# A hybrid decoder layer in split fp32: two output column blocks by seven products, with their weight sums made during the attention heads

## The chip, the cores and the metric

The kernel runs on one core of one Trainium2 chip. Its time is the device time of one launch in microseconds (us); shown are medians over runs. A core has TensorE (PE, matmuls), VectorE (DVE), ScalarE (ACT), GpSimd (POOL) and SyncE (SP, which here only starts transfers). Each engine works through its own instructions in a fixed order and waits on semaphores of the others.

## The reference, cut to what matters

S = 256 tokens, D = 2048, 16 heads, everything fp32.

```python
h = rmsnorm(x, pre_norm_g); proj = h @ w_in            # q_a, c_kv, k_rope, z, four conv parts, g_mla, g_conv
q = rmsnorm(q_a) @ w_q_b; kv = rmsnorm(c_kv) @ w_kv_b  # 16 heads, 128 + 64 rope
attn = causal_softmax(q k^T) v * silu(z);  y_mla  = attn @ w_o_mla
conv = sum(conv_w[k] * shifted(c_gate * c_in))
y_conv = (b_gate * conv * silu(z_conv)) @ w_o_conv
merged = sigmoid(g_mla) * y_mla + sigmoid(g_conv) * y_conv
out = merged @ w_out
x = x + rmsnorm(out, post_norm_g)
```

## The kernel before, in words

**Split fp32.** A product of fp32 matrices is made as three matmuls of rounded parts: hi x hi, lo x hi, hi x lo. Weights arrive as *raw units* of 128x2048 fp32 (1 MB): 4 blocks of 128 rows by 512 columns. A unit is rounded by `split_act`: ScalarE copies it into the rounded type (`whi`, L265), VectorE subtracts that from the raw values (`wlo`, L266). This is done in two halves of 1024 columns, into five half-sized buffers each for `whi` and `wlo`. The unit then serves 24 matmuls of 128x512: two row tiles of 128 tokens times four row blocks times three. All matmuls go through one helper (L88), which keeps them in program order; so the order of TensorE is the order of the code.

**The order of the other engines.** A scheduler arranges the instructions that are not marked `keep_in_program_order` by a simulated timeline when the kernel is built; the compiled order is then fixed. Raw units are loaded on SyncE's queue, three ahead (`ahead`), into three raw buffers, and rounded one ahead.

**Stages.** (1) Latents of the queries and keys, to 53 us. (2) Sixteen heads, to 590 us. Each head takes four weight units for the convolution channels (`cv`), with gates `z` for every fourth head, query and key units (`qn`, `kn`, `qr`) for every second head, and value units (`vv`) for every fourth; scores `sc`, `sw`, softmax `p` on VectorE and ScalarE, the probabilities turned by a round trip through DRAM, rounded as `pt`, and the values `o`. A head is one pass of a loop that calls, at fixed places, a generator that makes other data a step at a time (`make_forms`, for the next stage). `at_f` and `cv_f` hold the attention and convolution results of all heads, of 16 blocks each, and fill up head by head; `at_both`, `cv_both` are their rounded forms. (3) The gates, 590 to 916 us: four sets, each of two column blocks of both weights by *seven products* instead of eight (Strassen's scheme in Winograd's form: sums of weight blocks times sums of activation blocks, the latter being the *forms*), mixed with plain units `sq` of the branch outputs. A set's units are summed in place by VectorE (L1272, 128x2048) and rounded as `shi`, `slo`. (4) The output projection with `w_out`, 916.35 to 1003.39 us: 16 raw units in four column blocks c = 0..3 of 512, two row tiles, in the order of `out_order`; the merged activations `m` come back from DRAM turned (`turned_m`) and are rounded as `m_both`. (5) The norm, the gain, the residual and the stores.

Of the kernel before, what the change touches and what calls it, by code (L numbers as in the profile page):

```python
# [18 lines left out]
P = 128  # L19
S = 256  # L20
# [62 lines left out]
def tile_layer(ctx: ExitStack, tc: tile.TileContext, xw, w0, xb, x, pos, pvec, post_g, wc, wz, wcv, wkr, wqk, wqr, wv, cwr, wsq, out):  # L83
# [60 lines left out]

    out_order = [(0, 0), (0, 1), (1, 0), (1, 1), (0, 2), (1, 2), (0, 3), (1, 3)]
    out_order += [(c, k) for c in (2, 3) for k in range(4)]
    u_out = {ck: add(wsq[4, ck[0], ck[1]]) for ck in out_order}

    raws, splits, early = {}, {}, {}
    done = {"raw": 0, "split": 0, "end": u_first[1] + 1}  # L150

    def load_raw(i):
        ap, w = plan[i]
        t = early.get(i)
        if t is None:
# [20 lines left out]
    def split_unit(i):  # L176
        t, w = raws.pop(i), plan[i][1]
        parts = []
        if i == u_kr:
            t = t[:, :w].rearrange("p (k c) -> p k c", k=KD)  # L180
            for h in range(2):
                both = wpool.tile([P, HALF], F32R, name=f"whi{i}_{h}", tag="whi", bufs=5)
                both = both[:, :].rearrange("p (k j c) -> p k j c", k=KD // 2, j=2)
                ks = slice(h * KD // 2, (h + 1) * KD // 2)
# [4 lines left out]
        if i <= u_qa[-1]:  # L189

            hi, lo = (wpool.tile([P, HALF], F32R, name=f"{o}{i}", tag=o, bufs=5) for o in ("whi", "wlo"))
            for j in range(2):
# [4 lines left out]
            splits[i] = [(hi, lo)]  # L197
            return
        for h in range(0, w, HALF):
            n = min(HALF, w - h)  # L200
            if u_out[3, 0] <= i < u_out[3, 3]:
                both = spool.tile([P, 2, HALF], F32R, name=f"whl{i}_{h}", tag=LAST[len(last_parts)], bufs=1)
                last_parts.append(both)
                hi, lo = both[:, 0, :], both[:, 1, :]
            else:
                hi = wpool.tile([P, HALF], F32R, name=f"whi{i}_{h}", tag="whi", bufs=5)
                lo = wpool.tile([P, HALF], F32R, name=f"wlo{i}_{h}", tag="wlo", bufs=5)
            split_act(hi[:, :n], lo[:, :n], t[:, h : h + n], i in (u_head[0][1], *u_first, *u_d[0][2][:2]), i in (u_grp["r", 0], u_grp["v", 0], u_head[0][0]))
            parts.append((hi, lo))
# [13 lines left out]
    def take(i):  # L223
        ahead(i)
        return pieces(splits.pop(i))
# [391 lines left out]
    def group_a(g, together=False):  # L617
# [251 lines left out]
    def make_forms():  # L869
# [49 lines left out]
        while True:  # L919
            yield  # L920

    form, sums = {}, {}

# [6 lines left out]

    form_steps = make_forms()
    tap, coming, ps_by_head = None, [], {}
# [12 lines left out]

    def turned_unit(far, both, first, tag=None, queue=nc.sync):

# [3 lines left out]
        def load():  # L951
            name = f"turned_{both.name}{first}"
            if tag:
# [13 lines left out]

        return [[load if i == 0 else None, split(i), None, None] for i in range(len(far))]

# [24 lines left out]
    for h in range(H):  # L994
# [73 lines left out]
        if h < H - 2:  # L1068
            next(form_steps)
        channels(h, 2)  # L1070
        if h < H - 2:
            next(form_steps)
        if h == H - 1:
            split_branch(1)
# [49 lines left out]
    spool = right.enter_context(tc.tile_pool(name="spool", bufs=1, side="right", reuse_waits="tile"))  # L1124
    LAST = ("f5", "f6", "rb0", "rc0", "rc1", "rb1")
    last_parts = []

# [122 lines left out]
    def paired(i, n, c, combine):  # L1250
# [14 lines left out]
        def split(name, u, src, plus, then):  # L1265
            def go():
# [4 lines left out]
                if plus:  # L1271
                    nc.vector.tensor_tensor(t[:, :], t[:, :], raw[plus][:, :], op=ALU.add)  # L1272
                out = []
                for h in range(2):
                    hi = wpool.tile([P, HALF], F32R, name=f"shi{i}_{name}{u}_{h}", tag="whi", bufs=5)
                    lo = wpool.tile([P, HALF], F32R, name=f"slo{i}_{name}{u}_{h}", tag="wlo", bufs=5)
                    split_act(hi[:, :], lo[:, :], t[:, h * HALF : (h + 1) * HALF])
                    out.append((hi, lo))
                if then:
                    add_by_transfer(raw[then[0], u], then[1], 2 + u)  # L1280
                return pieces(out)
            return go
# [91 lines left out]
    m_b = Late("m", lambda i: spool.tile([P, 4, 2 * S], F32R, name=f"m_both{i}", tag=M_TAGS[i], bufs=1))  # L1374
    m_load = [turned_unit(far_m[a:b], m_b, a, tag, nc.gpsimd) for a, b, tag in ((0, 2, "rc0"), (2, 3, "rc1"), (3, 4, "rb1"))]

# [60 lines left out]
    loads.sort(key=lambda l: (max(l[1], -1), l[0]))  # L1437
    ns = 0
    ready = {}
    for j in range(-1, len(seq)):  # L1440
        while loads and loads[0][1] <= j:
            loads.pop(0)[2]()
        if j < 0:
            continue
        while ns < min(j + 3, len(seq)):
            ready[ns] = seq[ns][1]()
            ns += 1
        now[0] = j
# [3 lines left out]
        w = ready.pop(j)  # L1452
        if seq[j][2]:
            seq[j][2](w)
        for fn in pending.pop(j, []):
# [10 lines left out]
    assert not wanted and not fetched  # L1466

    m_load[1][0][0]()
    last_m = m_load[2][0]
# [9 lines left out]

    pss = [[bank(f"out{c}_{t}") for t in range(NT)] for c in range(2)]  # L1480
    for i, (c, kk) in enumerate(out_order[:4]):
        w = take(u_out[c, kk])
        if i == 0:
            last_m[0]()
        elif i == 2:
            m_load[1][0][1]()
        out_products(pss[c], w, kk)
    main.close()


    op = ctx.enter_context(tc.tile_pool(name="op", bufs=1))
    xr = op.tile([P, NT, D], F32, name="xr")
    og = op.tile([P, NT, D], F32, name="og")
    gb = op.tile([P, D], F32, name="gb")
    nc.scalar.dma_start(out=gb[:, :], in_=post_g.to_broadcast([P, D]))

    def out_block(c, t, ps):
# [5 lines left out]
        og_now = nc.vector.tensor_tensor(og[:, t, cs], ps[:, :], gb[:, cs], op=ALU.mult)  # L1503
        if c == 3:
            tc.keep_in_program_order(og_now)

# [48 lines left out]

    for i, (c, kk) in enumerate(out_order[4:6]):
        w = take(u_out[c, kk])
        if i == 0:
            last_m[1]()
        out_products(pss[c], w, kk)  # L1560
    tc.keep_in_program_order(nc.sync.dma_start(out=xr[:, :, :], in_=x))
    for c in range(3):
        if c == 2:
            pss.append([bank(f"out{c}_{t}") for t in range(NT)])
        for kk in range(4) if c == 2 else (3,):
            out_products(pss[c], take(u_out[c, kk]), kk)
        for t in range(NT):
            out_block(c, t, pss[c][t])
    nc.vector.reduce_sum(part[:, :], ssq[:, :, :3], axis=mybir.AxisListType.X)
    nc.vector.tensor_scalar(part[:, :], part[:, :], 1.0 / D, EPS, op0=ALU.mult, op1=ALU.add)  # L1570
    pss = [bank(f"out3_{t}") for t in range(NT)]
    for t in range(NT):
        for kk in range(4):
            if t == 0:
                last.append(take(u_out[3, kk]))
            out_products(pss, last[kk], kk, (t,))
        ps = out_block(3, t, pss[t])
        finish_by_two(t, ps) if t else finish(t)
# [90 lines left out]
```

## Time and profile before

| | |
|---|---|
| median of 3 runs | 1013.83 us (1013.68 to 1014.23) |
| the profiled execution | 1013.55 us, span 1011.8 us |
| granted TensorE clock | 0.998 |
| busy share of the span | PE 99%, DVE 80%, ACT 58%, POOL 17% |
| DMA | 261.84 MB, mean 259 GB/s |
| last output matmul ends | 1003.4 us; the end is the norm and the stores |

How to read the rows: in a group row, the line, the engine, the operation, out<-in with shape and count, then "busy us, mean ns of one", then the idle time of the engine just before them and what ended it. A timeline row has its start, its duration, the engine and what ran ("x2" joins two in a row), and in brackets the idle time before it with its cause. A window row has its limits, its length, the busy time of the engine asked for with the count of instructions, the granted clock, the share of the DMA engines and GB/s. Matmul rows overlap: the next starts before the end of the one before.

### The profile page before, as it was taken

To read this page: it belongs to the slowest core of one execution; us is meant where nothing else is said; L and a number is where in the kernel's file an instruction comes from. 1 tells how busy PE (TensorE), PEld (TensorE's weight loads), DVE (VectorE), ACT (ScalarE), POOL (GpSimd) and SP (SyncE) were. 2 spreads that over 40 slices of the span, in tenths; PEclk is the share of its full clock that TensorE was granted. 3 is DMA by queue.
4 is the path that set the end of the run, shared out by engine and by line. 5 is a ranking of instruction groups with operands and counts; after the bars stand their busy time and mean duration, and the time that the engine had idled before them with its cause. 6 is when DMAs were issued, how large, how long until landed. Compare 5 with 4: busy or idle time off the path is not lost.

```text
span 1011.8 us, 12983 instructions
## 1 busy us (share of the span) xinstructions
PE 1004.2 (99%) x4552; PEld 835.4 (83%) x4552; DVE 811.4 (80%) x1111; ACT 586.3 (58%) x838; POOL 170.7 (17%) x311
## 2 busy tenths in 40 slices
PE   9999999999999999999999999999999999999997
PEld 7888888888888888888888888888888888888886
DVE  7588878868888689877797889898989779997562
ACT  7675656556556456555565465565675664674541
POOL 4620411113211223212133110000000001003000
PEclk9999999999999999999999999999999999999999
DMA  8785768568786668866689779897599989639742
GB/s 338 282 291 183 260 201 304 197 214 276 234 303 232 228 229 283 272 219 232 216 264 338 292 306 291 344 375 218 187 333 296 305 321 260 239 127 322 289 166 84
DMA packets 54369, 261.84 MB, mean 259 GB/s; under 512 B 8768, under 2 KB 13504, under 8 KB 29216
## 3 DMA queue, kind: packets, MB, share of 16 engines
q1 hardware_dynamic: 37728, 214.35, 57.7%
q0 software_dynamic: 12256, 38.13, 14.0%
q10 hardware_dynamic: 4320, 8.54, 2.4%
q8 instruction: 35, 0.57, 0.2%
q14 instruction: 30, 0.25, 0.1%
HBM read 234.80 MB, written 22.02 MB: 254 GB/s over the span
## 4 chain that ended last, share of the span: by engine, by line
PE 98%; DMA 1%; DVE 0%; ACT 0%; SPq 0%; issue 0%
PE cv L88 34%; PE sq L88 17%; PE sX L88 9%; PE z L88 9%; PE out L88 9%; PE sZ L88 4%; PE kn L88 2%; PE qn L88 2%; PE vv L88 2%; PE sY L88 2%; PE ckv L88 2%; PE qa L88 2%; PE qr L88 1%; PE o L88 1%; PE sw L88 1%; DMA raw<-xb_dram 1%
## 5 line engine op out<-in xcount | busy, mean ns | idle before, releaser
L265 ACT ACTIVATE whi<-raw 128x1024 fp32r<-128x1024 f32 (+1 forms) x302 | 306.1, 1028 | 236.7 <-PE cv L88 103.9
L266 DVE TENSOR_TENSOR wlo<-raw,whi 128x1024 fp32r<-128x1024 f32 (+1 forms) x300 | 352.7, 1188 | 101.2 <-ACT whi L265 74.6
L88 PE MATMUL cv<-whi,x_both 128*128 128x512 f32 x1024 | 319.8, 389 | 0.0
L88 PEld LDWEIGHTS cv<-whi,x_both 128*128 128x128 f32 x1024 | 192.3, 188 | 39.5
L88 PE MATMUL cv<-wlo,x_both 128*128 128x512 f32 x512 | 199.5, 390 | 0.0
L88 PEld LDWEIGHTS cv<-wlo,x_both 128*128 128x128 f32 x512 | 96.2, 188 | 19.4
L266 DVE TENSOR_TENSOR slo_V<-b,shi_V 128x1024 fp32r<-128x1024 f32 x60 | 71.5, 1218 | 15.9 <-PE sq L88 8.5
L265 ACT ACTIVATE shi_V<-b 128x1024 fp32r<-128x1024 f32 x60 | 61.5, 1053 | 39.2 <-PE sq L88 21.2
L88 PE MATMUL z<-whi,x_both 128*128 128x512 f32 x256 | 80.0, 389 | 0.0
L366 POOL DMA_DIRECT2D far<-via x64 | 35.4, 559 | 227.2 <-DVE via L358 217.2
L88 PE MATMUL sq<-whi,at_both 128*128 128x512 f32 x256 | 60.6, 389 | 0.0
L88 PE MATMUL sq<-whi,cv_both 128*128 128x512 f32 x256 | 60.6, 389 | 0.0
L88 PEld LDWEIGHTS sq<-whi,cv_both 128*128 128x128 f32 x256 | 48.0, 188 | 10.0
L88 PEld LDWEIGHTS sq<-whi,at_both 128*128 128x128 f32 x256 | 48.0, 188 | 10.0
L88 PEld LDWEIGHTS z<-whi,x_both 128*128 128x128 f32 x256 | 48.1, 188 | 9.9
L88 PE MATMUL z<-wlo,x_both 128*128 128x512 f32 x128 | 49.8, 389 | 0.0
L88 PE MATMUL out<-whi,m_both 128*128 128x512 f32 x208 | 49.4, 389 | 0.0
L88 PE MATMUL sX<-shi_V,form 128*128 128x512 f32 x192 | 47.4, 389 | 0.0
L88 PEld LDWEIGHTS out<-whi,m_both 128*128 128x128 f32 x208 | 39.0, 188 | 8.1
L88 PEld LDWEIGHTS sX<-shi_V,form 128*128 128x128 f32 x192 | 36.0, 188 | 7.5
L265 ACT ACTIVATE shi_Q<-b 128x1024 fp32r<-128x1024 f32 x28 | 28.8, 1052 | 21.5 <-PE sq L88 19.1
L1263 POOL DMA_DIRECT2D b<-wsq_dram x8 | 7.0, 869 | 193.4 <-DVE b L1272 76.8
(304 smaller groups left out, 1568.7 us busy)
## 6 DMA issues: line engine op xcount, KB each, us to landing
raw<-wcv_dram SPq DMA_DIRECT2D x64, 1024.0 KB, 6.2
raw<-wsq_dram SPq DMA_DIRECT2D x48, 1024.0 KB, 7.2
b<-wsq_dram SPq DMA_DIRECT2D x26, 1024.0 KB, 5.7
raw<-wz_dram SPq DMA_DIRECT2D x16, 1024.0 KB, 4.9
raw<-wqk_dram SPq DMA_DIRECT2D x8, 1024.0 KB, 6.8
b<-wsq_dram POOLq DMA_DIRECT2D x8, 1024.0 KB, 11.0
far_form<-form ACTq DMA_DIRECT2D x28, 256.0 KB, 3.3
form<-far_form SPq DMA_DIRECT2D x7, 1024.0 KB, 13.8
```

Source lines behind the costliest of these rows:

```text
L88: return tc.keep_in_program_order(nc.tensor.matmul(*a, **kw))
L265: a = nc.scalar.activation(hi, src, AF.Copy)
L266: b = nc.vector.tensor_tensor(lo, src, hi.bitcast(F32), op=ALU.subtract)
L366: tc.keep_in_program_order(queue.dma_start(out=f[i], in_=m))
L1263: tc.keep_in_program_order(nc.gpsimd.dma_start(out=dst[:, :], in_=wsq[n, c + b, k], accum_op=ALU.add))
```

## The change

*Output projection.* Column blocks c = 1 and 2 are now made together by seven products (Q1, V5, V6, V7, V3, V4, Q2), each of two units of 12 matmuls, in three accumulators X, Z, Y. V5, V6, V7, V4 use weight sums. The activations' side needs four sums of `m` (the m forms V7, V5, V6, V3), made singly by VectorE and ScalarE in this stage. `out_order` has 22 units instead of 16; 8 of them are read from the weight sums (`far_sum`).

*Weight sums* (`make_sums`). Between heads 1 and 6, one step at each of three places in a head: 16 loads of 0.5 MB on SyncE's queue, 16 VectorE additions of 128x1024, 16 stores of 0.5 MB to DRAM on ScalarE's queue. They work in the quarters of `at_f` and `cv_f` that the heads have not filled yet.

*Whole-unit roundings.* From the end of the heads on, a unit is rounded by one ScalarE and one VectorE instruction of 128x2048 instead of two of 1024, in an area of five half slots used in turn; a pair that wraps takes slots 0 and 4. Only the first plain unit of the gate stage (raw115) is still rounded in halves, the first before the last head's values, the second after.

*Order.* In the gate stage the matmuls of a unit are issued before the rounding of the unit two ahead. In the first head the value unit no longer draws the rounding of the next unit (raw20) ahead. In the output stage five raw units are loaded ahead, six through a second area (`spare`), and all roundings are kept in program order. The rows `m2` and `m3` share a buffer, and the residual `xr` is loaded late.

Where the compiled order moves, before and after. Numbers at the end of names differ between the builds; `wlo_86` and `whi_85` are the five-slot areas.

VectorE, first head, from the rounding of the queries on. Before:

```order
L434 TENSOR_TENSOR f_867<-qn0_1_843,half_868 128x256
L266 TENSOR_TENSOR wlo20_0_874<-raw20_828,whi20_0_873 128x1024
L266 TENSOR_TENSOR wlo20_1024_878<-raw20_828,whi20_1024_877 128x1024
L266 TENSOR_TENSOR qn_lo_853<-f_863,qn_hi_852 128x256
L266 TENSOR_TENSOR qn_lo_853<-f_867,qn_hi_852 128x256
L434 TENSOR_TENSOR f_903<-kn0_0_885,half_904 128x256
```

After:

```order
L558 TENSOR_TENSOR f_867<-rp_a_871,rp_b_872 128x256
L312 TENSOR_TENSOR qr_862<-f_867,qr_862 64x256 x2
L312 TENSOR_TENSOR wlo_86<-raw20_784,whi_85 128x1024 x2
L312 TENSOR_TENSOR vv_lo_884<-vv0_0_889,vv_hi_883 128x512
L312 TENSOR_TENSOR vv_lo_884<-vv0_1_904,vv_hi_883 128x512
L312 TENSOR_TENSOR wlo_86<-raw21_821,whi_85 128x1024 x2
```

The roundings of raw20 have moved from ahead of the queries and keys to behind the rotated queries (`qr`).

VectorE, heads 5 to 6, from the queries to the rounded keys (`kn_... <- f_...`) of the next pair of heads. Before:

```order
L266 TENSOR_TENSOR wlo56_0_2785<-raw56_2698,whi56_0_2784 128x1024
L266 TENSOR_TENSOR qn_lo_2646<-f_2656,qn_hi_2645 128x256
L266 TENSOR_TENSOR qn_lo_2646<-f_2662,qn_hi_2645 128x256
L434 TENSOR_TENSOR f_2686<-kn3_0_2668,half_2687 128x256
L434 TENSOR_TENSOR f_2692<-kn3_1_2669,half_2693 128x256
L806 SCALAR_TENSOR_TENSOR cv_f_110<-cv5_0_2499,r_both_97,cv_f_110 128x512
L266 TENSOR_TENSOR kn_2647<-f_2686,kn_2647 128x256
L266 TENSOR_TENSOR kn_2647<-f_2692,kn_2647 128x256
L266 TENSOR_TENSOR wlo56_1024_2789<-raw56_2698,whi56_1024_2788 128x1024
```

After (L987 are the weight sums):

```order
L312 TENSOR_TENSOR wlo_86<-raw56_2557,whi_85 128x1024
L480 TENSOR_TENSOR f_2545<-kn3_0_2527,half_2546 128x256
L312 TENSOR_TENSOR wlo_86<-raw56_2557,whi_85 128x1024
L852 SCALAR_TENSOR_TENSOR cv_f_120<-cv5_1_2367,r_both_107,cv_f_120 128x512
L312 TENSOR_TENSOR qn_lo_2505<-f_2521,qn_hi_2504 128x256
L944 TENSOR_TENSOR form12_1_2668<-x_area_951,form12_1_2668 128x2x128
L937 TENSOR_TENSOR form_sum0_952<-x_area_951 128x256
L987 TENSOR_TENSOR cv_f_120<-at_f_119,cv_f_120 128x1024
L312 TENSOR_TENSOR kn_2506<-f_2545,kn_2506 128x256
```

The second half of raw56, two form steps and a weight sum now stand ahead of the first rounded keys; five more sums stand in the 44 rows before these.

ScalarE, end of the heads and start of the gate stage; `first_rt` are the first set's weights, which V5 adds to, `at_both3` the last quarter of the rounded attention result. Before:

```order
L811 ACTIVATE cg_5723<-cv15_1_5542,r_both_97 128x512
L265 ACTIVATE whi115_0_5729<-raw115_5727 128x1024
L265 ACTIVATE whi115_1024_5733<-raw115_5727 128x1024
L265 ACTIVATE at_both3_5747<-at_f_109 128x4x128 x2
L265 ACTIVATE whi116_0_5814<-raw116_5789 128x1024
L265 ACTIVATE whi116_1024_5818<-raw116_5789 128x1024
L1310 ACTIVATE sa0_5834<-sX0_5798 128x512
L265 ACTIVATE whi117_0_5838<-raw117_5791 128x1024
L265 ACTIVATE whi117_1024_5842<-raw117_5791 128x1024
L265 ACTIVATE whi118_0_5874<-raw118_5811 128x1024
L265 ACTIVATE whi118_1024_5878<-raw118_5811 128x1024
L265 ACTIVATE shi0_V50_0_5910<-first_rt0_5283 128x1024
```

After:

```order
L857 ACTIVATE cg_5351<-cv15_1_5194,r_both_107 128x512
L311 ACTIVATE whi_85<-raw115_5355 128x1024
L311 ACTIVATE at_both3_5369<-at_f_119 128x4x128 x2
L311 ACTIVATE whi_85<-raw115_5355 128x1024
L311 ACTIVATE whi_85<-raw116_5411 128x2048
L1402 ACTIVATE sa0_5452<-sX0_5420 128x512
L311 ACTIVATE whi_85<-raw117_5413 128x2048
L311 ACTIVATE whi_85<-first_rt0_4951 128x2048
L311 ACTIVATE whi_85<-raw118_5435 128x2048
```

`at_both3` has moved between the halves of raw115, and V5's rounding (of `first_rt0`) ahead of raw118's.

The diff, cut to its core:

```diff
@@ rounding of a unit @@
+    PARTS = 5
+    part_area = {o: wpool.tile([P, PARTS, HALF], F32R, name=o) for o in ("whi", "wlo")}
+    def unit_part(o):
+        a, b = sorted((part_n[o] + j) % PARTS for j in range(2))
+        part_n[o] += 2
+        return part_area[o][:, a : b + 1 : b - a, :]
...
+        if i == u_d[0][2][0]:
+            for h in range(len(halves[i]), 2):
+                if h == 0 or not only_first:
+                    hi, lo = half_part("whi"), half_part("wlo")
+                    split_act(hi, lo, t[:, h * HALF : (h + 1) * HALF], keep)
...
+        if i >= u_first[0]:
...
+                hi, lo = unit_part("whi"), unit_part("wlo")
+            split_act(hi[:, :, :], lo[:, :, :], t[:, :].rearrange("p (h s) -> p h s", h=2), keep, later)
@@ first head @@
-            ahead(u_grp["v", 0])
+            ahead(u_grp["v", 0], split=0)
@@ weight sums, one step a yield @@
+        for i in range(4):
+            bring(i, (3,))
+            plus(a, a, b)
+            yield
+            plus(b, b, c)
+            put(i, (1,))
+            yield
+            plus(c, a, c)
+            put(i, (0,))
+            if i < 3:
+                bring(i + 1, (0, 1))
+            yield
+            plus(d, c, d)
+            put(i, (2, 3))
+            if i < 3:
+                bring(i + 1, (2,))
+            yield
@@ a head, three places @@
             next(form_steps)
+            next(sum_steps)
@@ last head @@
-            split_unit(done["split"])
-            done.update(raw=done["raw"] + 1, split=done["split"] + 1)
+            split_unit(done["split"], True)
+            done["raw"] += 1
             finish_all(values(h, pt))
@@ output stage @@
+    def m_sum(i, j, x, y, op):
+        o = m_sums[:, i, 4 * j : 4 * j + 4, :]
+        tc.keep_in_program_order(nc.vector.tensor_tensor(quarters(o), x, y, op=op))
...
+    then((0, 0), last_m[0])
+    then((0, 1), form_of("V7"))
+    then((3, 0))
+    then(("Q1", 0))
+    then(("Q1", 1), lambda: m_load[1][0][1](True))
+    then((0, 2), form_of("V5"))
+    then(("V5", 0), lambda: last_m[1](True))
+    then(("V5", 1))
+    then((0, 3), lambda: copied("a", "X", "d"), form_of("V6"))
+    then(("V6", 0), lambda: copied("c", "Z", "a"))
+    then(("V6", 1), lambda: out_block(0, 0, pss[0][0]))
+    then((3, 1), lambda: out_block(0, 1, pss[0][1]))
+    then(("V7", 0), lambda: copied("b", "X", "b"), form_of("V3"))
+    then(("V7", 1))
+    then(("V3", 0))
+    then(("V3", 1), lambda: added("c", "X"))
+    then(("V4", 0), lambda: out_block(2, 1, res["c"], -1.0))
+    then(("V4", 1), lambda: added("b", "Z"), get_xr)
+    then(("Q2", 0), lambda: out_block(2, 0, res["b"], -1.0))
+    then(("Q2", 1), lambda: out_block(1, 1, set_bank["X"]))
```

Here `then(unit, steps)` first rounds the next unit (`take`), then does the steps, then issues the matmuls of the unit.

More of the change, by code (lines that the diff above doesn't have):

```diff
@@ L189, in split_unit @@
         if i <= u_qa[-1]:
-            hi, lo = (wpool.tile([P, HALF], F32R, name=f"{o}{i}", tag=o, bufs=5) for o in ("whi", "wlo"))
+            hi, lo = (half_part(o) for o in ("whi", "wlo"))
             for j in range(2):
@@ L223, in take @@
     def take(i):
-        ahead(i)
+        ahead(i, raw=5 if i >= u_out[0, 0] else 3)
         return pieces(splits.pop(i))
@@ L920, in make_forms, with make_sums, bring, put @@
             yield
+    def make_sums():
+        keep = tc.keep_in_program_order
+        area = [f[:, 4 * i : 4 * i + 4, :].rearrange("p k s -> p (k s)") for f in (at_f, cv_f) for i in (2, 3)]
+        a, b, c, d = area
+        w = 4 * S
+        def bring(i, which):
+            u, h = divmod(i, 2)
+            for n in which:
+                blk, k = ((1, u), (2, u), (2, 2 + u), (1, 2 + u))[n]
+                keep(nc.sync.dma_start(out=area[n], in_=wsq[4, blk, k][:, h * w : (h + 1) * w]))
+        def put(i, which):
+            u, h = divmod(i, 2)
+            for n in which:
+                keep(nc.scalar.dma_start(out=far_sum[("V5", "V7", "V6", "V4")[n], u][:, h * w : (h + 1) * w], in_=area[n]))
+        def plus(o, x, y):
+            keep(nc.vector.tensor_tensor(o, x, y, op=ALU.add))
+        for _ in range(3):
+            yield
+        bring(0, (0, 1))
+        bring(0, (2,))
+        yield
[10 more added lines that the diff above has]
+                bring(i + 1, (0, 1))
+            yield
+            plus(d, c, d)
+            put(i, (2, 3))
+            if i < 3:
+                bring(i + 1, (2,))
+            yield
+        while True:
+            yield
     form, sums = {}, {}
@@ L944, in score, with turned_unit @@
         return rest if later else rest()
-    def turned_unit(far, both, first, tag=None, queue=nc.sync):
+    def turned_unit(far, both, first, tag=None, queue=nc.sync, shared=None):
         box = []
@@ L966, in split @@
             return go
-        return [[load if i == 0 else None, split(i), None, None] for i in range(len(far))]
+        return [[load if i == 0 else None, split(i), None, None, box] for i in range(len(far))]
     def split_turned(src, both, t, keep=False):
@@ L1069, in tile_layer @@
             next(form_steps)
+            next(sum_steps)
         channels(h, 2)
@@ L1272, in go @@
                     nc.vector.tensor_tensor(t[:, :], t[:, :], raw[plus][:, :], op=ALU.add)
[L1273 to L1278, printed above, removed]
+                hi, lo = unit_part("whi"), unit_part("wlo")
+                split_act(hi[:, :, :], lo[:, :, :], t[:, :].rearrange("p (h s) -> p h s", h=2))
                 if then:
                     add_by_transfer(raw[then[0], u], then[1], 2 + u)
-                return pieces(out)
+                return pieces(by_halves(hi, lo))
             return go
@@ L1437, in tile_layer @@
     loads.sort(key=lambda l: (max(l[1], -1), l[0]))
-    ns = 0
-    ready = {}
+    ready = {ns: seq[ns][1]() for ns in range(2)}
+    ns = 2
     for j in range(-1, len(seq)):
@@ L1444, in tile_layer @@
             continue
+        w = ready.pop(j)
+        if seq[j][2]:
+            seq[j][2](w)
+        now[0] = j
         while ns < min(j + 3, len(seq)):
@@ L1478, in out_products @@
         ])
[L1480 to L1487, printed above, removed]
+    pss = {c: [bank(f"out{c}_{t}") for t in range(NT)] for c in (0, 3)}
+    m_raw = lambda blk, t: by_rows((m_01[0] if blk < 2 else pair_23)[:, (blk % 2) * 1024 + t * 512 :][:, :512], 4)
+    m_form = {n: spool.tile([P, KH, 2, P], F32R, name=f"m_form{n}", tag=tag, bufs=1) for n, tag in (("V5", "f5"), ("V6", "f6"), ("V7", "rb0"))}
@@ L1554, in finish_by_two @@
         store(t, 1536, 2048, og[:, t, cs])
[L1556 to L1568, printed above, removed]
+    res = {}
@@ new lines, in copied, with added, then @@
+    def copied(name, b, tag):
+        res[name] = wide(f"o{name}", tag)
+        tc.keep_in_program_order(nc.scalar.activation(res[name][:, :], set_bank[b][:, :], AF.Copy))
+    def added(name, b):
+        tc.keep_in_program_order(nc.vector.tensor_tensor(res[name][:, :], res[name][:, :], set_bank[b][:, :], op=ALU.add))
+    def then(n, *steps):
+        made = list(map(lambda f: f, steps))
+        c, k = n
+        w = take(u_out[n])
+        for f in made:
+            f()
+        if c in BANKS:
+            set_products(n, w)
+        else:
+            out_products(pss[c], w, k)
```

157 lines of the change are left out of this document (121 added, 36 removed).

## The prediction

> **What bounds the kernel now.** I read the page's busy shares first, then the waits of TensorE, then the chain of work that ended last, then the stretches around each edit.
>
> ```profile
> span 1011.8 us, 12983 instructions
> PE 1004.2 (99%) x4552; PEld 835.4 (83%) x4552; DVE 811.4 (80%) x1111; ACT 586.3 (58%) x838; POOL 170.7 (17%) x311
> q1 hardware_dynamic: 37728, 214.35, 57.7%
> PE 98%; DMA 1%; DVE 0%; ACT 0%; SPq 0%; issue 0%
> ```
> ```profile
> PE fin L88 <- ACT dg L1541: 0.9, 1, 0.9
> PE idle L88 <- PEq L1657: 0.8, 1, 0.8
> PE qa L88 <- ACT whi L265: 0.6, 2, 0.3
> ```
> ```profile
> 916.51 87.05 PE out L88 x384
> ```
>
> TensorE is the bound and waits 2.3 us in all, at the very start and end. The last row, of the chain, prices a matmul: 87.05 / 384 = 0.2267 us; a unit of 24 lasts 5.44, one of 12 lasts 2.72. So any matmul removed is worth 0.2267, and any work that comes late for TensorE is paid in full, unless it comes early enough to be hidden. Beside it VectorE is the fullest engine; its share of 80% is a mean, and the question is its queue where the change adds to it or reorders it.
>
> The prices of VectorE and ScalarE, by form:
>
> ```profile
> L266 DVE TENSOR_TENSOR wlo<-raw,whi 128x1024 fp32r<-128x1024 f32 x282 | 340.8, 1220 | 101.1 <-ACT whi L265 74.6 <-PE out L88 19.3 <-PE sY L88 1.8
> L1272 DVE TENSOR_TENSOR b<-b,b 128x2048 f32<-128x2048 f32 x16 | 36.5, 2283 | 0.3 <-DMA b<-wsq_dram 0.3
> L266 DVE TENSOR_TENSOR m_both<-turned_m,m_both 128x512 fp32r<-128x512 f32 x8 | 5.3, 684 | 1.4 <-ACT m_both L265 1.4
> L266 DVE TENSOR_TENSOR kn<-f,kn 128x256 fp32r<-128x256 f32 x16 | 6.3, 417 | 0.2 <-ACT kn L265 0.2
> L265 ACT ACTIVATE whi<-raw 128x1024 fp32r<-128x1024 f32 x282 | 294.0, 1057 | 233.0 <-PE cv L88 103.9 <-PE z L88 31.6 <-PE out L88 24.4
> ```
>
> Back to back each VectorE instruction starts about 0.08 before the one before ends (two 128x1024 in 2.34 to 2.36, quoted below), so in a queue a half costs 1.13 to 1.14, a whole 2.2, a 128x512 0.60, a 128x256 0.33. ScalarE's two halves take 1.99 together; a whole I estimate at 1.93.
>
> **The change, part by part.** I follow each engine's new order (the compiled orders, cut in the sections above) and put the durations of before on it. Times are those of before's trace.
>
> *Removed*: 384 matmuls of the output stage become 360: 24 x 0.2267 = **-5.44**. Nothing hides it; it is TensorE's own time.
>
> *A, first head.* The roundings of raw20 now stand behind the whole query and key chain on VectorE; before, they stood ahead of it.
>
> ```profile
> 81.01 2.34 DVE L266 TENSOR_TENSOR wlo<-raw,whi 128x1024 fp32r<-128x1024 f32 x2
> 89.13 0.87 DVE L266 TENSOR_TENSOR qr<-f,qr 64x256 fp32r<-64x256 f32 x2 [0.48 <-ACT qr L265]
> 87.34 0.39 PE L88 MATMUL cv<-wlo,x_both 128*128 128x512 f32 x1
> ```
>
> The chain ends at 90.0; with the two roundings (2.26) gone from ahead of it, at 87.7; the first half of raw20 then lands at 88.9 to 89.2, against 87.34: **+1.7** (0 if the scheduler's chain runs earlier, 2.3 if its keys wait).
>
> *B and D, the weight sums.* 16 additions of 128x1024 (16 x 1.13 = 18.1 us of VectorE) spread over heads 1 to 6. Nearly everywhere VectorE's gaps hide them. Not in front of the scores of head 6, which wait for the rounded keys:
>
> ```profile
> 245.00:274.29 29.29, 25.59 (x46) 1.00 0.71 245
> 272.41 0.75 DVE L266 TENSOR_TENSOR kn<-f,kn 128x256 fp32r<-128x256 f32 x2
> 274.26 0.28 PE L88 MATMUL sc<-kn,qn_hi 128*128 128x256 f32 x1
> ```
>
> (The first row is VectorE's busy time in a stretch.) Now stand ahead of the keys six sums (6.8) and, moved forward, half a rounding (1.13), two form steps (0.66) and a convolution product (0.66), less one 0.33: 8.9. The stretch has 29.29 - 25.59 = 3.7 idle, the lead of the keys included. 8.9 - 3.7 = 5.2 if every gap is filled; I take **+4.9**, since the chain there begins a little early (bounds 2, if half the sums slide into earlier gaps, and 7.5, if only the 1.4 of lead counts). B is a small one: one sum puts off a product that frees an accumulator in head 2, **+0.5** (0 to 1.1, one sum).
>
> *C, head 3.* The low part of the probabilities (pt) now stands behind both halves of raw44.
>
> ```profile
> 208.73 1.06 ACT L265 ACTIVATE whi<-raw 128x1024 fp32r<-128x1024 f32 x1 [3.01 <-PE z L88]
> 209.83 2.59 DVE L266 TENSOR_TENSOR wlo<-raw,whi 128x1024 fp32r<-128x1024 f32 x2 [2.85 <-ACT whi L265]
> 209.89 0.39 PE L88 MATMUL o<-pt,vv_hi 128*128 128x512 f32 x1
> ```
>
> In the new ring of five slots raw44's second half takes the slot that TensorE gives up at 208.7: ScalarE to 209.8, VectorE to 211.0, pt at 211.5, against 209.89: **+1.6** (0 to 3.1, the latter if the slot is the one that came free at 210).
>
> *E, end of the heads.* Only half of raw115 is rounded ahead of the last values; ScalarE does the second half behind at_both3, which waits for VectorE's at_f.
>
> ```profile
> 593.73 1.99 ACT L265 ACTIVATE whi<-raw 128x1024 fp32r<-128x1024 f32 x2
> 595.67 1.15 ACT L265 ACTIVATE at_both<-at_f 128x512 fp32r<-128x512 f32 x2
> 595.23 0.41 DVE L745 TENSOR_TENSOR at_f<-f,at_f 128x256 f32<-128x256 f32 x1
> 595.39 3.79 PE L88 MATMUL sq<-whi,at_both 128*128 128x512 f32 x16
> ```
>
> The second half is needed at the fifth of these matmuls, 596.3. at_f ended at 595.64 and is now about 1.1 later, because a whole rounding (2.2) stands where a half stood: 596.7 + 1.15 + 1.06 = 598.9, **+2.7** (1.5 if at_f is not later, 3.1 if it loses one thing more).
>
> *F.* ScalarE now rounds V5's sum ahead of raw118.
>
> ```profile
> 606.27 3.79 PE L88 MATMUL sq<-whi,at_both 128*128 128x512 f32 x16
> 605.97 4.48 DVE L1272 TENSOR_TENSOR first_rt<-first_rt,first_rb 128x2048 f32<-128x2048 f32 x2
> 611.71 3.79 PE L88 MATMUL sq<-whi,at_both 128*128 128x512 f32 x16
> ```
>
> V5's rounding takes a slot that TensorE gives up after 12 of the matmuls at 606.27, at 609.0; two whole units later (3.86) raw118 is there at 612.9, against 611.71: 1.2. VectorE follows with V5's low part, an addition (2.2) and only then raw118's: another 1.4. **+2.6** (1.2 to 3.9).
>
> *G, the gate stage.* Whole-unit roundings save VectorE some 0.07 each, but a unit's first half is ready 0.9 later on ScalarE and 1.1 later on VectorE.
>
> ```profile
> 850.00:900.00 50.00, 47.18 (x42) 1.00 0.65 208
> ```
>
> With 2.8 us free in 50 little is caught up. Following the order, two places come late, V4 of the second set (1.2) and V3 of the fourth (0.4): **+1.6** (0, the gain of VectorE covering it, to 3).
>
> *H, the output stage.*
>
> ```profile
> 916.00:960.00 44.00, 26.06 (x29) 1.00 0.84 306
> 960.00:1003.00 43.00, 21.44 (x26) 1.00 0.34 123
> ```
>
> VectorE had half its time free here; now it rounds 22 units instead of 16 and makes four forms (two 128x512 sums, 1.2, and a low part, 1.15, each, behind 1.06 of ScalarE). In the run of eight 12-matmul units (8 x 2.72 = 21.8) VectorE needs 8 x 2.2 + 2.35 + three additions and two gains (5 x 0.6) = 23.0. Each form is issued behind the next unit's rounding. V5's first unit starts at 916.35 + 27.2 = 943.6; its rounding waits for a slot until 937.2, ends on VectorE at 941.4, the sums at 942.6, ScalarE 943.7, the low part 944.9, against 943.8: 1.1. In the same way V6 0.9, V3 0.75 on ScalarE and 0.45 on VectorE, V4's first matmul 1.4 (its accumulator is read by an addition queued behind two roundings), small ones 0.3: **+4.9** (1.4, VectorE's excess alone, to 6.5).
>
> *DMA.* 6 MB more in the output stage fit the second row's share of 0.34. The sums add 16 loads and 16 stores of 0.5 MB (16.8 MB) to heads 1 to 6:
>
> ```profile
> 120.00:300.00 180.00, 145.97 (x247) 1.00 0.73 247
> raw<-wcv_dram SPq DMA_DIRECT2D x64, 1024.0 KB, 6.2
> ```
>
> q1 moved 214.35 MB in 57.7% of 1011.8 us, 367 GB/s, so they need 46 us of engine time; 0.27 x 180 = 49 is free. I cost it at nothing: a unit is asked for three units ahead (16.3 us) and lands in 6.2, so some 7 us of lead is left after both roundings. The price without that cover is the third rival.
> [...]
>
> Sum: 1.7 + 0.5 + 4.9 + 1.6 + 2.7 + 2.6 + 1.6 + 4.9 = 20.5; less 5.44: +15.1. The profiled execution took 1013.55, 0.3 under the median: **1028.6**.
>
> **Rivals.**
> *First, faster*: all waits are absorbed, since TensorE stalled nowhere before and a stall once paid gives every later queue its lead back; then only the 24 matmuls show: 1013.55 - 5.44 = 1008.1. For it: VectorE idles 20%. Against it: A, C, E and F are inversions in an order, not lack of throughput.
> *Second, no change*: only the inversions are real (A and C as costed, E and F at their low ends: 1.7 + 1.6 + 1.5 + 1.2 = 6.0) and the terms of load, D, G and H, vanish in gaps: 1013.55 - 5.44 + 6.0 = 1014.1. For it: the output stage's two rows show half of VectorE's time free. Against it: in front of the keys and in the gate stage the gaps are counted above and too short.
> *Third, slower still*: DMA saturates in heads 1 to 6. With 46 of 49 us taken, loads queue behind sums; it decides once a raw unit lands over 13 us after its issue. If a fifth of the 46 us reaches TensorE, 9 us: 1038.
>
> **How the numbers follow.** Forecast 0.58, first rival 0.12, second 0.13, third 0.17. The likeliest's own range, with the terms moving half independently, is 1022 to 1034. The range leaves out the first rival and the end of the third: **1013 to 1038**. About 0.2% (2 us) can be told from no change: faster 0.14 (the first rival and an edge of the second), same 0.06, slower 0.80.
>
> **What would show it.** Waits of TensorE by releaser in the profile after: one near 88 on VectorE's wlo, one near 212 on pt, the longest, near 280, on kn, one near 600 on ScalarE's whi, two on raw118, and five or six of about 1 us in the output stage on form parts; TensorE's last output matmul some 15 us later than 1003.4, with 24 fewer of them. I am wrong if TensorE's waits sum to under 6 us, if waits on DMA lead the list, or if the stall at kn is missing while DVE's sums are there.

## The result, and the profile after

The changed kernel takes 1036.1 us (median of 5, 1035.32 to 1038.91) against 1013.68 (1013.36 to 1014.23): 1.0226 times, 95% interval 1.0212 to 1.024, 22.4 us slower. The forecast was 1028.6, in a range of 1013 to 1038: direction and range held, the size was 15 of 22.

Two lines of the page, then TensorE's waits (engine, tile, releaser, us in total, times, longest):

```profile
span 1034.3 us, 12660 instructions
PE 1005.5 (97%) x4528; PEld 831.5 (80%) x4528; DVE 847.2 (82%) x1045; ACT 592.8 (57%) x748; POOL 170.9 (17%) x311
```
```profile
PE sc L88 <- DVE kn L312: 7.5, 1, 7.5
PE sq L88 <- ACT whi L311: 5.2, 3, 2.2
PE o L88 <- DVE pt L312: 1.6, 1, 1.6
PE cv L88 <- DVE wlo L312: 1.6, 1, 1.6
PE sq L88 <- DVE wlo L312: 1.5, 1, 1.5
PE out_setX L88 <- DVE oc L1711: 1.2, 1, 1.2
...
PE out_setZ L88 <- DVE m_formV L1595: 0.8, 1, 0.8
PE out_setX L88 <- DVE m_formV L1597: 0.8, 1, 0.8
PE out_setZ L88 <- ACT whi L311: 0.6, 1, 0.6
```

The waits are where the forecast put them: the keys (kn), pt, raw20's wlo, raw115 and raw118, the forms. Yet the listed waits come to some 21.7 us, less 5.4 for the matmuls: 16. The rest of the 22.4 is in PE's busy time. It rose from 1004.2 to 1005.5 with 24 matmuls fewer. So matmuls ran slower somewhere.

TensorE's order up to the output stage did not change, so the n-th matmul of one trace can be set against the n-th of the other. The growth of the difference of their starts, place by place (a restart costs 0.1 to 0.3 more than the wait in the list):

| place (time before) | forecast | measured | run that bears on it |
|---|---|---|---|
| A, raw20, 87 | 1.7 | 1.8 | e6 |
| B, head 2, 144 | 0.5 | 0.6 | e1, e3 |
| C, pt, 210 | 1.6 | 1.8 | e1 |
| D, keys of head 6, 274 | 4.9 | 7.6 | e1, e2, e3 |
| slow clock after D | none | 2.5 | e11, e12 |
| E, raw115, 596 | 2.7 | 2.5 | e6 |
| F, raw118, 612 | 2.6 | 3.2 | e4, e5 |
| G, V4 and V3 of the sets | 1.6 | 0.2 | |
| sq, 758 | none | 2.1 | e1, e2, e3 |
| H, output stage | 4.9 | 5.9 | e4 |
| 24 matmuls | -5.4 | -5.4 | |
| start of the latents, and small steps | none | -0.5 | |
| sum | 15.1 | 22.3 | |

The two profiled executions differ by 22.5 us. The start of the latents is a difference between launches: it is -0.9 in e12, whose code there is that of before.

*D and the clock.* TensorE's timeline at the keys, then the granted clock (the fourth number) in windows of TensorE:

```profile
285.52 0.58 PE L88 MATMUL sc<-kn,qn_hi 128*128 128x256 f32 x1 [7.47 <-DVE kn L312]
...
287.82 0.63 PE L88 MATMUL cv<-wlo,x_both 128*128 128x512 f32 x1
...
291.96 0.39 PE L88 MATMUL cv<-wlo,x_both 128*128 128x512 f32 x1
```
```profile
286.00:291.00 5.00, 5.00 (x15) 0.52 0.64 219
291.00:295.00 4.00, 4.00 (x19) 1.00 0.83 157
```

After the wait TensorE runs some 5 us at half clock (0.63 for a matmul that otherwise shows 0.39). That is the 2.5 us.

VectorE had the six sums in front of the keys, as forecast, but it also stood still there, for 3.0 us in one piece. ScalarE's timeline and, under it, SyncE's issues and VectorE's window (the last two numbers: DMA share, GB/s) and timeline:

```profile
262.76 1.06 ACT L311 ACTIVATE whi<-raw 128x1024 fp32r<-128x1024 f32 x1 [1.94 <-DMA raw<-wcv_dram]
...
271.84 2.01 ACT L311 ACTIVATE whi<-raw 128x1024 fp32r<-128x1024 f32 x2 [5.64 <-DMA raw<-wcv_dram]
```
```profile
256.95 1.06 SPq L979 DMA_DIRECT2D at_f<-wsq_dram  x2
260.87 0.33 SPq L198 DMA_DIRECT2D raw<-wcv_dram  x1
```
```profile
263.00:272.00 9.00, 6.92 (x10) 1.00 1.03 402
```
```profile
272.93 2.36 DVE L312 TENSOR_TENSOR wlo<-raw,whi 128x1024 fp32r<-128x1024 f32 x2 [3.01 <-ACT whi L311]
```

A raw unit asked for at 260.87, behind two loads of the sums, landed near 271.8: 11 us, against a median of 6.2 before, while the DMA engines were full (share 1.03). That is the third rival's mechanism, inside the forecast's own place. The loads of the sums stand in the raw units' own queue, ahead of this one. The stores are in ScalarE's queue, and they moved at the same time: while the unit was on its way (260.87 to 271.76), SyncE's queue moved 2.70 MB, ScalarE's 1.18 MB and GpSimd's 0.53 MB.

*The wait at 758* (the time before; 780 after) has a late transfer in it too, long after the sums. ScalarE's row of before, then two of after, and a VectorE window:

```profile
752.96 1.16 ACT L265 ACTIVATE cv_both<-turned_cv 128x512 fp32r<-128x512 f32 x2 [0.25 <-DMA turned_cv<-far_cv]
```
```profile
777.09 1.15 ACT L311 ACTIVATE cv_both<-turned_cv 128x512 fp32r<-128x512 f32 x2 [4.92 <-DMA turned_cv<-far_cv]
778.15 1.89 ACT L311 ACTIVATE whi<-raw 128x2048 fp32r<-128x2048 f32 x1
```
```profile
767.00:778.00 11.00, 9.61 (x9) 1.00 0.99 378
```

A raw unit's rounding stands on ScalarE behind cv_both, which waits for a transfer. Before, the first half of that unit stood ahead of it; a whole unit can't. Full DMA engines alone are not what is new: their share in this stretch was 1.01 before (746 to 757 us). But the two transfers landed 9.9 and 11.0 us after their issue, against 6.9 and 7.8 before. In the profiles of e1 and e2 they took 9.0 to 10.4 and the wait cost 1.3; in e3's they took 6.6 and 7.4 and there was no wait, though no edit of these three touches this place. Why the transfers are late is not shown.

### The profile page after: what moved, and what is told of

It is laid out like the page before. It is cut to its first block, busy times and chain, and to the rows that moved or that the text cites. A ratio compares the mean times of both kernels' runs of the same rounds, so it can differ in the third digit from the quotient of the medians.

```text
span 1034.3 us, 12660 instructions
## 1 busy us (share of the span) xinstructions
PE 1005.5 (97%) x4528; PEld 831.5 (80%) x4528; DVE 847.2 (82%) x1045; ACT 592.8 (57%) x748; POOL 170.9 (17%) x311
## 5 line engine op out<-in xcount | busy, mean ns | idle before, releaser
L311 ACT ACTIVATE whi<-raw 128x1024 fp32r<-128x1024 f32 (+2 forms) x260 | 303.6, 1177 | 226.5 <-PE cv L88 100.0
L312 DVE TENSOR_TENSOR wlo<-raw,whi 128x1024 fp32r<-128x1024 f32 (+2 forms) x258 | 352.7, 1375 | 91.2 <-ACT whi L311 86.0
L311 ACT ACTIVATE whi<-b 128x2048 fp32r<-128x2048 f32 x44 | 84.5, 1920 | 62.1 <-PE sq L88 37.2
L312 DVE TENSOR_TENSOR wlo<-b,whi 128x2048 fp32r<-128x2048 f32 x44 | 100.3, 2289 | 20.5 <-ACT whi L311 13.0
L88 PE MATMUL sX<-whi,form 128*128 128x512 f32 x256 | 63.3, 389 | 0.0
L88 PEld LDWEIGHTS sX<-whi,form 128*128 128x128 f32 x256 | 48.0, 188 | 10.0
L1368 DVE TENSOR_TENSOR b<-b,b 128x2048 f32<-128x2048 f32 x16 | 36.6, 2286 | 1.8 <-DMA b<-wsq_dram 1.6
L88 PE MATMUL sX<-wlo,form 128*128 128x512 f32 x128 | 34.3, 390 | 0.0
L88 PE MATMUL sq<-wlo,at_both 128*128 128x512 f32 x128 | 31.8, 390 | 1.5 <-DVE wlo L312 1.5
```

The costliest lines, as they stand in the source:

```text
L88: return tc.keep_in_program_order(nc.tensor.matmul(*a, **kw))
L311: a = nc.scalar.activation(hi, src, AF.Copy)
L312: b = nc.vector.tensor_tensor(lo, src, hi.bitcast(F32), op=ALU.subtract)
```

## The experiments

All are edits of the changed kernel but e11 and e12, which are edits of the kernel before. e1, e2, e3 and e10 leave out the sums or a part of them, so they give times and not the layer's result. Times of before in the three groups of runs: 1012.98, 1013.17, 1013.21.

**e1: no sums.**

```diff
-            u_out[n, k] = add(far_sum[n, k][:, :])
+            u_out[n, k] = add(wsq[4, 1 if n in ("V5", "V4") else 2, k])
...
-    form_steps, sum_steps = make_forms(), make_sums()
+    form_steps, sum_steps = make_forms(), iter(lambda: 0, 1)
```

> The changed kernel without the weight sums: nothing of them is loaded, added or stored during the heads, and the output stage reads a plain block of w_out in place of each sum. If the sums are what delays head 2, head 3 and head 6 (waits of TensorE that grew its lateness by 0.6, 1.8 and 10.1 us, the slowed clock behind the last one included), all three go: 1036.1 - 12.5 = 1023.6. If these waits come from the order of the roundings and not from the sums, they stay: 1036. The waits in the gate and output stages stay in both cases.

1023.33 (1.0097, 1.0082 to 1.0113). B, C and D are gone: no wait between 90 and 590 us. So pt (C), which I had put down to the new order of the roundings alone, came from the sums too: without them the compiled order rounds pt earlier again. A, E, F and H are about what they were, but for a stretch of slow clock behind E in this profile (more in the last section).

**e2 and e3: additions only, transfers only.** The first two edits are e2's (with e1's first), the last is e3's.

```diff
-                keep(nc.sync.dma_start(out=area[n], in_=wsq[4, blk, k][:, h * w : (h + 1) * w]))
+                pass
...
-                keep(nc.scalar.dma_start(out=far_sum[...][:, h * w : (h + 1) * w], in_=area[n]))
+                pass
...
         def plus(o, x, y):
-            keep(nc.vector.tensor_tensor(o, x, y, op=ALU.add))
+            pass
```

> Only the 16 additions of the weight sums are left; they add what happens to lie in the areas, no sum is loaded or stored, and the output stage reads plain blocks. VectorE's load alone (the forecast): TensorE waits 5 us for the keys of head 6, instead of 7.5; about 1031. If the transfers alone made the wait: under 1 us for the keys, about 1025.

> The 16 loads and 16 stores of the weight sums stay, the 16 additions are left out, so what is stored is not a sum. If VectorE's load alone makes the wait for the keys of head 6, it falls under 1 us: about 1024. If the saturated DMA engines make it, a raw unit still lands 10 us or more after its issue between 250 and 275 us, and the wait for the keys stays at 3 us or more: about 1028.

1031.87 (1.0191, 1.0162 to 1.0219; one of the four launches took 1037.08) and 1031.82 (1.0186, 1.0164 to 1.0208). TensorE's longest wait in each, then VectorE's windows in front of it:

```profile
PE sc L88 <- DVE kn L312: 5.9, 1, 5.9
```
```profile
250.00:270.00 20.00, 19.87 (x29) 1.00 0.70 235
```
```profile
PE sc L88 <- DVE kn L312: 4.7, 1, 4.7
```
```profile
255.00:263.00 8.00, 6.06 (x12) 1.00 0.97 369
263.00:272.00 9.00, 5.05 (x9) 1.00 1.03 422
```

With the additions alone VectorE is full (19.87 of 20) at a DMA share of 0.70: the forecast's mechanism, 5.9 where it said 4.9. With the transfers alone VectorE has 3.9 us of 9 free and the DMA engines none: the rival's mechanism, 4.7. Each alone delays the keys by 5 to 6 us and brings the slow clock (a mean of 0.98 from 120 to 300 us in both, where before has 1.00); together they give 7.5. The two don't add; I take it that they meet in the same stretch of VectorE's queue, which the one fills and the other stops. Neither expectation of "under 1 us" held. C is gone in both runs, so it needs the additions and the transfers; B is gone in e3 alone, so it comes from an addition.

**e4: halves from free buffers.**

```diff
-        k = part_n[o] % PARTS
         part_n[o] += 1
-        return part_area[o][:, k, :]
+        return wpool.tile([P, HALF], F32R, name=f"{o}_{part_n[o]}", tag=o, bufs=PARTS)
...
-                hi, lo = unit_part("whi"), unit_part("wlo")
-            split_act(hi[:, :, :], lo[:, :, :], t[:, :].rearrange("p (h s) -> p h s", h=2), keep, later)
+            for h in range(2):
+                hi, lo = half_part("whi"), half_part("wlo")
+                split_act(hi[:, :], lo[:, :], t[:, h * HALF : (h + 1) * HALF], keep, later)
```

> Every rounding is made in two halves again, from five half buffers given out as they come free; all else is as in the changed kernel. The forecast put the output stage's waits on forms that queue behind the next unit's rounding: by that they stay near 5.9 us, and so does raw118's (2 to 3), for some 1033. If the whole unit is the cause (it needs two slots at once and gives its first half late), the waits of raw118 (3.2), at 758 us (2.1) and of the output stage (5.9) shrink to 1.5 in all, E stays at 2.2: 1036.1 - 0.3 - 9.7 = 1026.

1025.3 (1.0117, 1.0094 to 1.014). What is left behind 590 us:

```profile
PE sq L88 <- ACT whi L314: 1.4, 1, 1.4
PE out_setX L88 <- DVE oc L1717: 1.1, 1, 1.1
...
PE out_setX L88 <- DVE m_formV L1603: 0.4, 1, 0.4
```

F (3.2) and the wait at 758 (2.1) are gone, E falls from 2.5 to 1.7, and the output stage falls from 5.9 to 2.0 though every form still stands behind the next unit's rounding. The whole-unit rounding, not the forms' place, cost most of H. Of what is left there, 1.35 is V4's wait (oc, the addition that reads its accumulator), a matter of place as e7 shows, and 0.6 a form. The wait at 758 proves less: in this profile its transfers landed after 7.1 and 8.0 us, so nothing shows what halves do with late ones. The profiled launch (1028.15) is the slowest of the four, with 8.8 at D and 2.5 of slow clock (a mean of 0.97 from 120 to 300 us); behind 590 us it gains 10 us, close to the 10.8 between the medians.

**e5: halves, but slots in turn.** e4 with the first three lines undone (`part_area[o][:, k, :]`).

> Roundings in two halves again, but the five half slots are still taken strictly in turn, from one area. If the whole unit alone made the waits behind 590 us, this equals the run with halves and free buffers: 1025.3, no wait at raw118. If the turn of the slots makes raw118's wait (V5's rounding, put ahead of it, must have the slot that TensorE gives up last), that wait stays at 2.5 us while the one near 760 us and most of the output stage's are gone: 1027.5.

1030.69 (1.0169, 1.0155 to 1.0182). Raw118's waits are back, 2.75 us in all (its matmuls start 0.6 later at ScalarE's part, 1.8 at VectorE's, the rest are restarts); the gate stage and the output stage stay as in e4. The compiled orders differ too. In e5 ScalarE rounds V5's sum ahead of raw118, as in the changed kernel; in e4 raw118 comes first, as before. So the fixed turn of the slots came with the late order, and free buffers with the old one; no run has one without the other, and which of them costs F stays open. The median is 5.4 us above e4's, but the two profiles, with the same 8.8 us at D, differ by 2.6, which is F.

**e6: the old order in two places.** e4 with

```diff
-            ahead(u_grp["v", 0], split=0)
+            ahead(u_grp["v", 0])
...
-            split_unit(done["split"], True)
-            done["raw"] += 1
+            split_unit(done["split"])
+            done.update(raw=done["raw"] + 1, split=done["split"] + 1)
```

> Halves from free buffers, and the two orders of before besides: raw20 rounded ahead in the first head, raw115 rounded whole before the last values. If these two orders are what A and E are, TensorE's waits near 87 (2.3 us) and 600 us (1.7) go and nothing else: 1025.3 - 4.0 = 1021.3. If the first matmuls wait for the queue of VectorE in any order, they stay: 1025.

1020.89 (1.0076, 1.0062 to 1.0089), as expected. A and E are gone, and what is left is mostly the sums and V4:

```profile
PE sc L88 <- DVE kn L315: 6.7, 1, 6.7
PE o L88 <- DVE pt L315: 1.6, 1, 1.6
PE out_setX L88 <- DVE oc L1717: 1.1, 1, 1.1
```

**e7, e8, e9: the sums kept away from the keys.** e6 with V4's addition ahead of the next rounding, and steps of the sums left out at some places (they end later for it). In e7 (the first step shown is at a head's first place, the other at its second; e8 has heads 2, 3 and 5 in the first line):

```diff
+            if h not in (1, 2, 5):
                 next(sum_steps)
...
+            if h not in (5,):
                 next(sum_steps)
...
+        if n == ("V3", 1):
+            made.pop(0)()
         w = take(u_out[n])
```

e9 starts the sums in the first head and leaves out the first place of heads 1, 3, 5, the second of 5, and the third of 4 and 5.

> The kernel of the run before this one, with the weight sums kept away from where keys are made: no step at the first place of heads 1, 2 and 5 and at the second of head 5, so they end in head 7; and the addition that frees V4's accumulator is issued ahead of the next unit's rounding. If the six sums in front of head 6 and their transfers make the waits of heads 2, 3 and 6 and the slow clock after it (13 to 14 us there), these go, and V4's 1.3: 1021.3 - 15 = 1006, faster than before. If the DMA engines are full with the sums wherever they stand, raw units land late elsewhere in the heads: 1012 or more.

> As the run before, with the step of head 3 left out in place of head 1's. By the theory of places it is the same as that run within 0.2%: 1006. If the transfers matter, the two differ by more than 1 us and the rows name DMA as the releaser.

> As the spread kernel of before, but the sums start in the first head and no step of them stands between the last place of head 4 and the end of head 5, so neither an addition nor a transfer of theirs lies in front of the keys of head 6. If that place is what is left of their cost (a wait of 2 to 3 us and 1.5 of slow clock), it goes: 1006 to 1008. If the sums' 16.8 MB cost the same wherever they stand: 1011 again.

1012.23 (0.9989, 0.9978 to 1.0), 1010.74 (0.9982, 0.9968 to 0.9996) and 1012.24 (0.9992, 0.9978 to 1.0007). They win 9 to 10 us against e6, and none reaches 1006: e7 and e9 come out at the time of the second theory. e8's own question stays open: its median is 1.5 us under e7's, but the launches of each spread over more than 5 us, and TensorE's wait at the keys (2.9 in e7, 2.2 in e8) is released by VectorE in both. e8 just beats the kernel before. In e9 nothing is left at the keys, and the wait is elsewhere: first TensorE's, then VectorE's timeline, then a VectorE window.

```profile
PE cv L88 <- DVE vv_lo L315: 3.7, 1, 3.7
```
```profile
222.15 0.69 DVE L885 TENSOR_TENSOR mv<-mv,cw 128x512 f32<-128x512 f32 x1 [4.99 <-DMA cw<-cwr_dram]
...
210.00:220.00 10.00, 3.67 (x3) 1.00 0.99 306
```

With the DMA engines full (0.99), a small transfer for the convolution landed 12.3 us after its issue (a median of 6.5 in e10), and VectorE waited for it with the values' low part behind it. With the slow clock after it (a mean of 0.75 from 220 to 230 us) the wait cost 6.4 us. The twelve launches of e9 spread from 1008.53 to 1017.69, where the four of e10 without the sums stay within 1007.94 to 1008.65. So what the sums cost changes from launch to launch. That this comes from the DMA engines alone is not shown: e2, without transfers, has a launch 5 us above its others too.

**e10: the same without sums.** e7 with the edit of e1.

> The same kernel without the weight sums at all; the output stage reads a plain block of w_out in place of each. This is what the seven products are worth with the sums for nothing: 1013.2 - 5.4 + 0.6 of waits in the output stage = 1008.4 if that is all; if the sums cost nothing any more in the run before this one, the two are within 0.2%.

1008.28 (0.9948, 0.9935 to 0.9962), as worked out: the seven products are worth 5 us, and the sums, spread as well as I could, cost 2.5 to 4 of them.

**e11, e12: what a wait costs.** The kernel before, with the first key of heads 6 and 7 multiplied by 1, twelve times or twice, before it is rounded:

```diff
         for j, f in enumerate((k or keys())()):
+            for _ in range(12 if g == 3 and j == 0 else 0):
+                nc.vector.tensor_scalar(f[:, :], f[:, :], 1.0, None, op0=ALU.mult)
```

> The kernel before, with twelve multiplications by 1 of the first key of heads 6 and 7 on VectorE, which make TensorE wait some 7 us for it. If a wait costs its length: 1013.2 + 7 = 1020. If a long wait is followed by a slow clock, as seen after the one of 7.5 us: 2 to 3 more, 1022.7.

> As the run before, with two multiplications: a wait of about 2 us at the same place. If the slow clock needs a long wait, none follows, as after the wait of 2.2 us near 612 us: 1015.3. If the place decides (small matmuls for the scores follow it), 1 to 2 more: 1017.

1021.97 (1.0087, 1.0071 to 1.0104) and 1015.95 (1.0025, 1.0017 to 1.0034). The wait of 6.5 us set TensorE back by 8.5, of 2.0 by 2.3. TensorE's windows behind the wait in e11, then in e12:

```profile
280.00:283.00 3.00, 2.91 (x9) 0.50 0.91 204
283.00:287.00 4.00, 4.00 (x18) 0.89 0.09 27
```
```profile
276.00:278.00 2.00, 2.00 (x12) 1.00 0.93 328
278.00:281.00 3.00, 3.00 (x15) 1.00 0.91 300
```

So the long wait cost its length and a stretch at half clock; this one of 2.0 us cost its length, and 0.3 for the restart.

## Why the prediction was right, and where not

*The total.* The range held, but 1036.1 lies outside the likeliest's own range (1022 to 1034) and nearer to the third rival's 1038 than to 1028.6. That nearness is chance. What the sum lacked is 2.7 at D, 2.5 of slow clock, 2.1 at 758 and 1.0 at H, less 1.4 too much at G. Of these only D and the clock behind it carry the third rival's mechanism.

*What bounds the kernel* held: TensorE's own time fell by the 24 matmuls, and every late instruction that was not hidden came through in full.

*A, B, C, E, F* came from the compiled order with durations of before, and came out within 0.6 us each (9.9 measured, 9.1 forecast). e6 undoes A and E together, e4 F. For C the price was right and the cause too narrow: without the sums (e1), or with half of them (e2, e3), the order that put pt late does not arise.

*D* was under-sized: 4.9 against 7.6. The step that failed is the cost of the sums' DMA "at nothing". The count was not too low: it gave 46 us of engine time, and over the same matmuls (120 to 300 us before, 121 to 314 after) the DMA share rose from 0.73 to 0.87, which I estimate at 36 us. But it was a mean over 180 us; over 9 us before the keys the engines were full (1.03), and VectorE stood still for 3.0 of the 7.6 us. It should have been made stretch by stretch, as VectorE's count was. e3 shows that the transfers alone were enough for 4.7 us. The third rival's mechanism was real. Its limit of 13 us from issue to landing (10.9 did harm here), its price of 9 us more, and its being a rival at all and not a part of D, were wrong.

*The slow clock* (2.5) was left out. The step that failed is the sentence that late work is "paid in full": after the wait of 7.5 us TensorE itself was slower (a clock of 0.52 from 286 to 291 us), and the wait cost 2.5 us more than its length.

*G* was 1.6 at two places where 0.2 came, and 2.1 came at a third: the late transfer with a whole unit queued behind it. The reason given, that a whole unit's first half is ready late, fits the third place only in part: there the half could no longer go ahead of the transfer, and the transfer was late, which the forecast did not have.

*H* was near in size (4.9 against 5.9), with the wrong step named. "Each form is issued behind the next unit's rounding" is true in e4 as well, and there 2.0 is left. It was the whole rounding that left no time for the forms. How it did so stays open: it needs two slots at once, it gives its first half late, and the transfer of `m` that the V5 form needs landed 20.3 us into the stage, against 18.3 in e4. The V4 term (1.4 forecast, 1.4 measured) had its cause right: e7 moves that addition and the wait is gone.

*Second rival*: of its terms that were to vanish in gaps, G did (0.2); D and H did not (7.6 and 5.9).

*First rival*: its reason, that stalls are caught up, is refuted by the table: no lateness was ever won back. Its time, 1008.1, is what e10 shows once the waits are designed away (1008.28).

## What to carry to other kernels

Where TensorE has no gaps, fold the new instruction order onto the old durations, queue by queue; that priced five of these places to within 0.6 us. Do the same for the DMA engines, in windows as short as the lead of a load, because a mean share of 0.73 hides stretches that are already full (0.93 from 260 to 270 us in the kernel before). And a larger instruction that saves little time (0.07 us here) can cost much more where its two halves were started, released and used one at a time.

## What the runs showed of the hardware

Behind some of TensorE's waits the granted clock was half for a time. From 120 to 300 us its mean was 1.00 in before, e1 and e10, where TensorE has no such wait there, 0.98 in e9, e3 and e2 (waits of 3.7, 4.7 and 5.9 us) and 0.97 in the changed kernel and e4 (7.5 and 8.6 us). Beside the wait it cost 2.5 us at D, 2.0 in e11 (8.5 less 6.5) and 2.7 in e9 (6.4 less 3.7).

The length of the wait alone does not decide. The wait of 2.0 us in e12 was followed by a clock of 1.00 (276 to 285 us). The same kind of wait, 2.2 us long in e8, was followed by one of 0.57:

```profile
276.00:277.00 1.00, 1.00 (x6) 1.00 1.08 404
277.00:281.00 4.00, 4.00 (x12) 0.57 0.87 249
281.00:285.00 4.00, 4.00 (x19) 1.00 0.99 318
```

And E's wait for raw115 left the clock alone in the changed kernel (2.25 us; 1.00 from 612 to 620 us) but not in e1 (2.24 us), where the next twelve matmuls took 4.34 us (from 600.45 to 604.79) instead of the 2.72 of a unit of 12.

The profiler's records of the granted clock show where its changes lie. In the changed kernel's trace it falls to half at 280.53, is full again at 290.77 and falls at 1031.47; the distances are 10.24 and 740.69 us, 3 and 217 steps of 3.413 us. In the trace of before the two records, of full clock at 4.36 and of half at 1007.87, lie 1003.52 us apart, 294 such steps. Cut into windows of this step that end at the changes, with TensorE's idle time summed in each, the traces give at full clock (e8's change is at 277.40, from its clock of 0.70 between 277 and 278 us):

| run | wait | TensorE's idle time in the window (its start) | clock in the next window |
|---|---|---|---|
| after, E | 2.25 | 1.36 (608.21), then 0.89 | full |
| after, A | 1.6 | 1.56 (85.97) | full |
| e8 | 2.2 | 2.01 (273.98) | half |
| before, the end | 0.9, then no more matmuls | 2.28 (1004.46) | half |
| after, the end | no more matmuls | 2.41 (1028.05) | half |
| after, D | 7.5 | 2.48 (277.12) | half |

All other windows at full clock in the changed kernel's trace, from 4.05 us on, have at most 1.47 us of idle time, and full clock followed each. At half clock there, half followed the windows with 3.41 (280.53) and 1.58 (283.94), and full the one with none (287.35). My reading of these few rows is that E's wait did no harm because an edge of the windows cut it in two, and that e8's did because 2.01 of its 2.2 us fell into one. Where the edges lie in e12 and e1 is not shown here.
